# Attention over memory keys: a key tile of the sample comes in four transfers to all 128 partitions in place of two to 64 partitions each

## The chip, the core and the metric

The kernel runs on one core of one Trainium2 chip. The metric is the device time of one execution in microseconds (us); each execution loads all inputs from the chip's memory and stores all outputs. One step holds a prompt of 256 tokens and 8 sample sequences of 8 tokens, so 320 tokens in all, with a model width of 2048. All arrays are float32.

## What is computed

One layer of a hybrid decoder: a mixer (a state space scan and a short convolution), an attention over 256 memory tokens, and a lookup of experts (PEER), each added to the residual. The change touches the attention over the memory alone:

```python
def mem_attend(xn, k, v, wq, wo):
    b, L, _ = xn.shape
    q = (xn @ wq).reshape(b, L, MEM_HEADS, MEM_HEAD_DIM)
    s = jnp.einsum('blhd,bmhd->bhlm', q, k.astype(q.dtype)).astype(jnp.float32) * (1.0 / math.sqrt(MEM_HEAD_DIM))
    p = jax.nn.softmax(s, axis=-1)
...
```

There are 4 heads of 512 columns. The prompt's keys and values are computed by this kernel (stored as outputs `p_mem_k`, `p_mem_v`, and read back); those of the 8 sample sequences come from the inputs `cache_mem_k` and `cache_mem_v`, 256 tokens x 4 heads x 512 columns for each sequence. So one head of one sequence has a key block of 256 x 512 numbers, 512 KB, of which a row of 2 KB lies every 8 KB in memory.

## The kernel before

The program is one stream of work for the engines. TensorE (PE), VectorE (DVE) and ScalarE (ACT) run in an order that the kernel writes out by hand; the order of GpSimd (POOL), which in this stage only issues DMA transfers, is chosen by the framework's scheduler. Weights come through SyncE's own queue (SP).

In the attention stage the loop runs over four heads. A head has nine key tiles (eight of the sample, one of the prompt) and nine value tiles. Between them stand pieces of the projection of the next head's queries, and in the last head of the output projection (`between`, L1503 to L1507); the matmuls of these pieces are `pg` at L1214 to L1216.

A key or value tile is `kv`, 128 partitions x 1024 numbers (512 KB), made and loaded by `kv_load` (L1122). There are ten buffers (KVT): seven in a pool of their own, three in pool `PQ`. So a load waits until the tile ten places earlier has been used: a key tile is free after VectorE's transpose (`turned`, L1361 to L1363, written to `tt`), a value tile after TensorE's matmuls (L1448).

`kv_load(src, blocks)` has three forms. Sample keys (called at L1153 for the first head and at L1396 for the others) have `blocks` 2: two transfers, one for each half of the 512 columns, each to 64 partitions. Prompt keys (L1368) have `blocks` 4: four transfers to 32 partitions each. Values (L1368 and L1433) have `blocks` 0: one transfer to all 128 partitions. Sample keys and prompt keys are issued at L1129, values at L1132.

After the load VectorE transposes a key tile in blocks of 32 x 32 (L1363), TensorE multiplies it with the queries into the scores `pss` (sample, L1408) or, after a split in two parts, `psp` (prompt, L1424 to L1426), a softmax follows on a side stream, and the values are multiplied into `pso` (sample, L1448) and `po` (prompt, L1466 to L1468). L248 on ScalarE and L249 on VectorE make the two parts (H and L) of a float32 operand, for weights `W` as for keys. When the attention is done, POOL loads the residual again (`XN`, L1497), which was stored at L1157 (`x_d<-XF`).

The first eight key loads are queued before the stage (`open_kv`, L1149 to L1153): seven of them go out from 886 to 917 us, while the mixer's output projection runs, and the eighth at 1140 us.

Of other transfers on POOL the text names these: the stores of `row` at L740, of which the first four (417.9 to 420.3 us) read 3 partitions and write 72 runs of 32 numbers each, in the list of order 72x1x32; the loads and stores of the scan's state, `SB` (L778, L926, 128x8x128), and `EE` (L702, 64x16x64).

Of the kernel before, what the change touches and what calls it, by code (L numbers as in the profile page):

```python
# [23 lines left out]
TS = 64  # L24
# [139 lines left out]
def step(ctx, tc, ins, outs, dbg=None, stop=None):  # L164
    nc = tc.nc
# [956 lines left out]
    def kv_load(src, blocks):  # L1122
        def load():
            own = next(tiles) % KVT < KV1
            t = (KV if own else PQ)["pool"].tile([P, 1024], F32, tag="kv", bufs=KV1 if own else KVT - KV1, name="kv")
            if blocks:
                n, p = 512 // blocks, P // blocks
                for e in range(blocks):
                    nc.gpsimd.dma_start(t[p * e:p * e + p].rearrange("p (a d) -> p a d", d=n),  # L1129
                                        src[:, n * e:n * e + n].rearrange("(a p) d -> p a d", p=p))  # L1130
            else:
                nc.gpsimd.dma_start(t.rearrange("p (m d) -> p m d", m=2), src.rearrange("(m p) d -> p m d", p=P))  # L1132
            ready.append(t)
        loads.append(load)
# [1145 lines left out]
```

## Time and profile before

| quantity | value |
|---|---|
| time of three executions | 3087.83, 3092.4, 3096.58 us |
| median | 3092.4 us |
| time of the profiled execution | 3088.27 us |
| its span | 3086.5 us |
| granted TensorE clock over the span | 0.997 |
| attention stage, from the first prompt key load to the last value's matmul | 1141 to 1352 us |
| DMA traffic, mean over the span | 295 GB/s |

The profile is one execution. PE, DVE, ACT, POOL and SP are the engines TensorE, VectorE, ScalarE, GpSimd and SyncE; PEld is TensorE's loading of weights. The span is the time from the first to the last instruction; the execution's time is a little longer. A row of a group or of a timeline names the line of the program, the engine, the operation, and output <- input; in brackets or after the last bar stands how long the engine was idle before it, and the instruction or DMA whose end released it. `in_cache_mem_k_dram` and `in_cache_mem_v_dram` are the caches of the sample; `out_dram` as an input is the prompt's keys or values. A row of a DMA issue gives the KB of one transfer and the median time from issue to landing, in us. The granted clock is TensorE's, as a share of full speed.

### The profile page before, as it was taken

How to read it: one execution, taken by the hardware profiler on the slowest of the kernel's cores; microseconds unless marked ns; L12 is line 12 of the kernel's file. 1: busy time of each engine (PE TensorE's matmuls, PEld its weight loads, DVE VectorE, ACT ScalarE, POOL GpSimd, SP SyncE). 2: the span in 40 equal slices, each digit the busy share in tenths (PEclk: the TensorE clock that was granted, in tenths of full speed). 3: DMA queues.
4: the chain of work that ended last, by engine and by line, in shares of the span. 5: the costliest groups of instructions: out<-in, count | busy, mean ns of one | idle time of the engine just before them, and what ended most of it. 6: DMA issues, size and time to landing. Idle time of an engine off the chain costs nothing.

```text
span 3086.5 us, 55315 instructions
## 1 busy us (share of the span) xinstructions
PE 3051.7 (99%) x19709; PEld 2794.0 (91%) x19709; DVE 2275.2 (74%) x4477; ACT 1589.5 (51%) x3202; POOL 1359.7 (44%) x1500
## 2 busy tenths in 40 slices
PE   8999999999999999999999999999999999999998
PEld 7889999999999999889999999888888888888886
DVE  5556866666566456656778899988885889888886
ACT  5545643434554443444554444766674545555555
POOL 0011221111110002310458999989887656555553
PEclk9999999999999999999999999999999999999999
DMA  8888899899999858975966788879998999999996
GB/s 275 288 270 308 302 331 333 304 330 307 357 320 353 292 186 228 261 235 159 244 201 223 287 319 316 304 290 319 336 331 264 344 331 361 338 345 334 332 305 220
DMA packets 445321, 909.19 MB, mean 295 GB/s; under 512 B 43336, under 2 KB 252400, under 8 KB 419572
## 3 DMA queue, kind: packets, MB, share of 16 engines
q1 hardware_dynamic: 316372, 543.31, 51.3%
q0 software_dynamic: 60656, 227.34, 22.4%
q10 hardware_dynamic: 68016, 135.01, 12.8%
q8 instruction: 154, 2.52, 0.3%
q14 instruction: 123, 1.01, 0.1%
HBM read 849.44 MB, written 190.05 MB: 337 GB/s over the span
## 4 chain that ended last, share of the span: by engine, by line
PE 84%; issue 4%; DMA 3%; POOL 3%; DVE 3%; ACT 1%; SPq 0%; DVEq 0%; POOLq 0%; ACTq 0%
PE pg L371 11%; PE pg L372 11%; PE pg L373 11%; PE pu L1998 7%; PE acc L2173 6%; PE acc L2174 6%; PE acc L2172 6%; PE pu L1999 4%; POOL L L1979 3%; PE pu L2005 2%; PE pu L2004 2%; PE pu L2003 2%; PE pgate L1901 2%; PE pg L1214 2%; PE pg L319 1%
## 5 line engine op out<-in xcount | busy, mean ns | idle before, releaser
L249 DVE TENSOR_TENSOR L<-W,H 128x512 fp32r<-128x512 f32 x1312 | 899.2, 711 | 341.0 <-ACT H L248 332.0
L248 ACT ACTIVATE H<-W 128x512 fp32r<-128x512 f32 x1312 | 795.9, 628 | 679.6 <-PE acc L2174 234.7
L1979 POOL TENSOR_TENSOR L<-tt,H 128x512 fp32r<-128x512 f32 x511 | 646.8, 1298 | 60.7 <-ACT H L1976 50.0
L371 PE MATMUL pg<-AH,H 128*128 128x320 f32 x1856 | 581.7, 313 | 0.0
L373 PE MATMUL pg<-AH,L 128*128 128x320 f32 x1856 | 573.6, 309 | 0.0
L372 PE MATMUL pg<-AL,H 128*128 128x320 f32 x1856 | 573.4, 309 | 0.0
L2172 PE MATMUL acc<-H,wt 128*128 128x512 f32 x1024 | 398.5, 389 | 1.1 <-DVE at L2012 1.1
L2173 PE MATMUL acc<-L,wt 128*128 128x512 f32 x1024 | 398.8, 389 | 0.6 <-DVE L L249 0.5
L2174 PE MATMUL acc<-H,wt 128*128 128x512 f32 x1024 | 398.4, 389 | 0.0
L1976 ACT ACTIVATE H<-tt 128x512 fp32r<-128x512 f32 x512 | 309.0, 626 | 144.8 <-DVE tt L1967 120.0
L1967 DVE STREAM_TRANSPOSE tt<-W 128x512 f32<-128x512 f32 x512 | 338.1, 691 | 58.9 <-POOL L L1979 55.7
L1998 PE MATMUL pu<-XP,H 128*128 128x512 f32 x1035 | 371.2, 399 | 0.0
L371 PEld LDWEIGHTS pg<-AH,H 128*128 128x128 f32 x1856 | 349.0, 188 | 2.1 <-issue 0.5
L372 PEld LDWEIGHTS pg<-AL,H 128*128 128x128 f32 x1856 | 348.7, 188 | 1.8
L373 PEld LDWEIGHTS pg<-AH,L 128*128 128x128 f32 x1856 | 348.4, 188 | 0.0
L1999 PE MATMUL pu<-XP,L 128*128 128x256 f32 x1104 | 297.0, 279 | 0.3 <-POOL L L1979 0.3
L2121 POOL TENSOR_TENSOR at<-at,G 128x108 f32<-128x108 f32 x192 | 168.4, 891 | 252.0 <-DMA at<-act_d 205.0
L2005 PE MATMUL pu<-XP,L 128*128 128x256 f32 x944 | 269.4, 285 | 3.0 <-POOL L L1979 2.7
L2003 PE MATMUL pu<-XP,H 128*128 128x256 f32 x944 | 267.8, 284 | 0.1
L2004 PE MATMUL pu<-XP,H 128*128 128x256 f32 x944 | 267.0, 283 | 0.0
L1998 PEld LDWEIGHTS pu<-XP,H 128*128 128x128 f32 x1035 | 194.3, 188 | 39.9
L2173 PEld LDWEIGHTS acc<-L,wt 128*128 128x128 f32 x1024 | 192.2, 188 | 42.0 <-DVE L L249 2.1
(496 smaller groups left out, 5810.3 us busy)
## 6 DMA issues: line engine op xcount, KB each, us to landing
u_d<-in_peer_u_dram ACTq DMA_DIRECT2D x128, 1024.0 KB, 8.4
W<-u_d SPq DMA_DIRECT2D x128, 1024.0 KB, 6.6
W<-in_peer_v_dram SPq DMA_DIRECT2D x256, 512.0 KB, 6.4
W<-in_w_in_dram SPq DMA_DIRECT2D x176, 512.0 KB, 7.4
W<-in_w_out_dram SPq DMA_DIRECT2D x64, 512.0 KB, 6.5
W<-in_w_mem_k_dram SPq DMA_DIRECT2D x32, 512.0 KB, 5.9
W<-in_w_mem_v_dram SPq DMA_DIRECT2D x32, 512.0 KB, 5.6
kv<-in_cache_mem_k_dram POOLq DMA_DIRECT2D x64, 256.0 KB, 9.0
```

The costliest lines, as they stand in the source:

```text
L248: S.activation(h, src, AF.Copy)
L249: V.tensor_tensor(l, src, h.bitcast(F32), ALU.subtract)
L371: PE.matmul(out, hv[:, j, c0:c1], ah[:, k, 0:n], start=st, stop=False)
L372: PE.matmul(out, hv[:, j, c0:c1], al[:, k, 0:n], start=False, stop=False)
L373: PE.matmul(out, lv[:, j, c0:c1], ah[:, k, 0:n], start=False, stop=sp)
L1967: V.transpose(tt.rearrange("p (k a i) -> p k a i", a=4, i=32), box["x", i].rearrange("p (a k j) -> p k a j", a=4, k=16)[:, 4 * q:4 * q + 4])
L1979: G.tensor_tensor(l, src, h.bitcast(F32), ALU.subtract)
L1998: PE.matmul(*wide, start=k == 0, stop=False)
L1999: PE.matmul(pu[:, 0:TP], lv[:, j], PP["xp"][:, 0, k], start=False, stop=False)
L2172: PE.matmul(out, th, h, start=i == 0, stop=False)
L2173: PE.matmul(out, th, l, start=False, stop=False)
L2174: PE.matmul(out, tl, h, start=False, stop=i == P - 1)
```

## The change

`kv_load` gets a form of its own for `blocks` 2. A sample key tile now comes in four transfers in place of two. The tile's contents stay the same: partition 64 e + p, column 256 a + d holds row 64 a + p, column 256 e + d of the key block.

```diff
--- before.py
+++ after.py
@@ -1123,7 +1123,11 @@
         def load():
             own = next(tiles) % KVT < KV1
             t = (KV if own else PQ)["pool"].tile([P, 1024], F32, tag="kv", bufs=KV1 if own else KVT - KV1, name="kv")
-            if blocks:
+            if blocks == 2:
+                for a in range(4):
+                    nc.gpsimd.dma_start(t[:, 256 * a:256 * a + 256],
+                                        src[TS * a:TS * a + TS].rearrange("p (e d) -> e p d", e=2))
+            elif blocks:
                 n, p = 512 // blocks, P // blocks
                 for e in range(blocks):
                     nc.gpsimd.dma_start(t[p * e:p * e + p].rearrange("p (a d) -> p a d", d=n),
```

| | before | after |
|---|---|---|
| transfers of one sample key tile | 2 | 4 |
| bytes of one transfer | 256 KB | 128 KB |
| partitions written by one | 64 | 128 |
| runs of 1 KB per partition in one | 4 | 1 |
| source of one, outermost first | 64 rows, 4 row blocks, 256 numbers | 2 column halves, 64 rows, 256 numbers |

(TS is 64.) There are 32 sample key tiles. Lines behind L1125 of the program move down by four: the transfers of sample keys are at L1128 after the change, of prompt keys at L1133, of values at L1136. PE, DVE, ACT and SP keep their order, but for the numbers in the names of tiles.

On POOL each transfer waits for a semaphore of a ring of eight (DMASW0 to DMASW7), that is for the landing of the transfer eight places before it; the first transfer of a tile also waits for the engine that used the buffer (DVE or PE). Among the first keys of the last head, before the change (names: `kv` is a tile, the second name the input, then partitions x runs x numbers of one run as the list shows the tile's side):

```order
L1129 DMA kv_14285<-in_cache_mem_k_dram 64x4x256 [waits DMASW2_49,DVE_49]
L1129 DMA kv_14285<-in_cache_mem_k_dram 64x4x256 [waits DMASW3_49]
L1132 DMA kv_14344<-in_cache_mem_v_dram 128x2x512 [waits DMASW4_49,PE_49]
L1132 DMA kv_14354<-in_cache_mem_v_dram 128x2x512 [waits DMASW5_49,PE_49]
L1129 DMA kv_14379<-in_cache_mem_k_dram 64x4x256 [waits DMASW6_49,DVE_49]
L1129 DMA kv_14379<-in_cache_mem_k_dram 64x4x256 [waits DMASW7_49]
L1132 DMA kv_14402<-out_6_dram 128x2x512 [waits DMASW0_49,PE_49]
L1129 DMA kv_14439<-in_cache_mem_k_dram 64x4x256 [waits DMASW1_49,PE_49]
L1129 DMA kv_14439<-in_cache_mem_k_dram 64x4x256 [waits DMASW2_49]
```

After the change, at the same place:

```order
L1128 DMA kv_14433<-in_cache_mem_k_dram 128x1x256 [waits DMASW2_49,DVE_49]
L1128 DMA kv_14433<-in_cache_mem_k_dram 128x1x256 [waits DMASW3_49]
L1128 DMA kv_14433<-in_cache_mem_k_dram 128x1x256 [waits DMASW4_49]
L1136 DMA kv_14398<-in_cache_mem_v_dram 128x2x512 [waits DMASW5_49,PE_49]
L1136 DMA kv_14408<-in_cache_mem_v_dram 128x2x512 [waits DMASW6_49,PE_49]
L1128 DMA kv_14433<-in_cache_mem_k_dram 128x1x256 [waits DMASW7_49]
L1136 DMA kv_14458<-out_6_dram 128x2x512 [waits DMASW0_49,PE_49]
L1128 DMA kv_14495<-in_cache_mem_k_dram 128x1x256 [waits DMASW1_49,PE_49]
L1128 DMA kv_14495<-in_cache_mem_k_dram 128x1x256 [waits DMASW2_49]
L1128 DMA kv_14495<-in_cache_mem_k_dram 128x1x256 [waits DMASW3_49]
L1128 DMA kv_14495<-in_cache_mem_k_dram 128x1x256 [waits DMASW4_49]
L1128 DMA kv_14517<-in_cache_mem_k_dram 128x1x256 [waits DMASW5_49,DVE_49]
```

The three keys from kv_14433 on now pass through the ring in four steps each; two value loads that stood ahead of both steps of a key (kv_14344, kv_14354) stand ahead of its last step (kv_14398, kv_14408 ahead of the fourth of kv_14433).

The last two sample keys of the last head, before the change (the tile kv_14564 is the last one; two value loads follow, then the prompt's keys):

```order
L1132 DMA kv_14504<-in_cache_mem_v_dram 128x2x512 [waits DMASW6_49,PE_49]
L1129 DMA kv_14533<-in_cache_mem_k_dram 64x4x256 [waits DMASW7_49,PE_49]
L1129 DMA kv_14533<-in_cache_mem_k_dram 64x4x256 [waits DMASW0_49]
L1129 DMA kv_14564<-in_cache_mem_k_dram 64x4x256 [waits DMASW1_49,DVE_49]
L1129 DMA kv_14564<-in_cache_mem_k_dram 64x4x256 [waits DMASW2_49]
L1132 DMA kv_14581<-in_cache_mem_v_dram 128x2x512 [waits DMASW3_49,PE_49]
L1132 DMA kv_14615<-in_cache_mem_v_dram 128x2x512 [waits DMASW4_49,PE_49]
L1129 DMA kv_14643<-out_5_dram 32x8x128 [waits DMASW5_49,DVE_49]
L1129 DMA kv_14643<-out_5_dram 32x8x128 [waits DMASW6_49]
```

And after it:

```order
L1136 DMA kv_14564<-in_cache_mem_v_dram 128x2x512 [waits DMASW2_49,PE_49]
L1128 DMA kv_14593<-in_cache_mem_k_dram 128x1x256 [waits DMASW3_49,PE_49]
L1128 DMA kv_14593<-in_cache_mem_k_dram 128x1x256 [waits DMASW4_49]
L1128 DMA kv_14593<-in_cache_mem_k_dram 128x1x256 [waits DMASW5_49]
L1128 DMA kv_14593<-in_cache_mem_k_dram 128x1x256 [waits DMASW6_49]
L1128 DMA kv_14626<-in_cache_mem_k_dram 128x1x256 [waits DMASW7_49,DVE_49]
L1128 DMA kv_14626<-in_cache_mem_k_dram 128x1x256 [waits DMASW0_49]
L1128 DMA kv_14626<-in_cache_mem_k_dram 128x1x256 [waits DMASW1_49]
L1128 DMA kv_14626<-in_cache_mem_k_dram 128x1x256 [waits DMASW2_49]
L1133 DMA kv_14707<-out_5_dram 32x8x128 [waits DMASW3_49,DVE_49]
L1133 DMA kv_14707<-out_5_dram 32x8x128 [waits DMASW4_49]
L1136 DMA kv_14645<-in_cache_mem_v_dram 128x2x512 [waits DMASW5_49,PE_49]
```

Between two value loads stand eight steps of keys where four stood, which is the whole ring; the first prompt key step stands directly behind the last sample key, ahead of two value loads that stood before it.

## The prediction

> **What bounds the kernel now.** First the page's busy times and the windows of the attention stage.
>
> ```profile
> PE 3051.7 (99%) x19709; PEld 2794.0 (91%) x19709; DVE 2275.2 (74%) x4477; ACT 1589.5 (51%) x3202; POOL 1359.7 (44%) x1500
> ...
> 1140.00:1200.00 60.00, 60.00 (x503) 57.24 (x502) 36.93 (x70) 25.17 (x50) 14.69 (x24) 1.00 0.87 242
> 1200.00:1250.00 50.00, 49.37 (x447) 42.46 (x447) 33.05 (x56) 22.21 (x55) 17.50 (x27) 1.00 0.81 224
> 1250.00:1300.00 50.00, 49.29 (x469) 41.44 (x467) 31.97 (x55) 19.58 (x48) 17.52 (x27) 1.00 1.04 271
> 1300.00:1350.00 50.00, 43.68 (x378) 33.46 (x377) 27.73 (x48) 19.86 (x45) 16.18 (x24) 0.90 0.93 286
> ```
>
> A window's columns are its length, then busy PE, PEld, DVE, ACT, POOL, the granted clock, the DMA share and GB/s. TensorE is the bound: it is idle 0.63, 0.71 and 6.32 us in the last three windows and never in the first. So the changed loads can gain only in the last, and can lose wherever they make TensorE wait. What ended the waits, from the waits of PE over the stage, its timeline and VectorE's:
>
> ```profile
> PE pss L1408 <- DVE tt L1363: 3.2, 1, 3.2
> PE pg L1215 <- DVE AL L249: 2.9, 1, 2.9
> ...
> 1321.69 0.47 PE L1216 MATMUL pg<-AH,L 128*128 128x320 f32 x1
> 1326.83 0.31 PE L1216 MATMUL pg<-AH,L 128*128 128x320 f32 x1
> ...
> 1306.07 1.25 DVE L1363 STREAM_TRANSPOSE tt<-kv 128x1024 f32<-128x1024 f32 x1 [0.29 <-DMA kv<-in_cache_mem_k_dram]
> 1315.46 1.25 DVE L1363 STREAM_TRANSPOSE tt<-kv 128x1024 f32<-128x1024 f32 x1 [4.46 <-DMA kv<-in_cache_mem_k_dram]
> 1318.46 1.25 DVE L1363 STREAM_TRANSPOSE tt<-kv 128x1024 f32<-128x1024 f32 x1 [1.75 <-DMA kv<-in_cache_mem_k_dram]
> ```
>
> The first wait is TensorE's for a transposed key tile, and that transpose had waited 4.46 us for a key load; the second is for a split behind the next late transpose (VectorE runs in order). Both are the key load. They cost 3.2 + 2.9 = 6.1 us. Then the clock: over those 50 us it was 0.90, which is 0.10 x 50 / 0.5 = 10 us at half speed (the same matmul 0.47 us instead of 0.31); less the 2.9 us idle among them, 7 us of work ran at half and lost 3.5 us. **If the key loads came early, 6.1 + 3.5 = 9.6 us would go; that is the most this change can gain.** The chain of waits, in order of time, says why the load is late:
>
> ```profile
> 1303.13 0.61 POOL kv L1129
> 1303.75 14.59 DMA kv<-in_cache_mem_k_dram
> 1318.52 1.11 issue
> ```
>
> It was issued at 1303 and took 14.6 us. It could not be issued earlier: in the list of order each load waits for the landing of the one eight places before it. Eight transfers are in flight at most, so a stretch of n transfers with landing time L takes n x L / 8.
>
> **What is unchanged.** VectorE, ScalarE, TensorE and SyncE keep their instructions and order; bytes and destinations are the same. Three things change: issues on POOL, how a transfer is dealt to the DMA engines and memory, and the number of loads in that line of eight.
>
> **1. Issues.** 32 sample key tiles, two more transfers each, 64 in all. The page's groups and the lines of POOL by form have these durations:
>
> ```profile
> L1129 POOL DMA_DIRECT2D kv<-in_cache_mem_k_dram x64 | 39.7, 627 | 90.7 <-DVE tt L1363 41.6 <-DVE XS L1076 23.2 <-PE pt L241 8.9
> L1132 POOL DMA_DIRECT2D kv<-in_cache_mem_v_dram x32 | 22.9, 717 | 62.4 <-DVE tt L1363 32.4 <-PE pso L1448 14.5 <-DMA kv<-in_cache_mem_k_dram 5.8
> L926 POOL DMA_DIRECT2D out_dram<-SB x16 | 14.6, 915 | 104.4 <-DVE SB L922 99.1 <-DVE L L249 5.4
> L1129 POOL DMA_DIRECT2D kv<-out_dram x16 | 9.4, 591 | 10.9 <-DMA kv<-in_cache_mem_k_dram 4.1 <-DVE AL L249 3.2 <-DVE tt L1363 1.8
> L1157 POOL DMA_DIRECT2D x_d<-XF x8 | 4.4, 548 | 217.2 <-DVE XF L1113 217.2
> ...
> L702 POOL DMA_DIRECT2D EE<-acs_d x2 | 1.7, 834 | 2.1 <-DMA acs_d<-ACS 2.1
> ...
> L740 POOL DMA_DIRECT2D out_dram<-row x4 | 2.6, 665 | 0.0
> ```
>
> (The last row is of the window 417.8 to 420.3 us.) The new load moves 128 runs of 1 KB, as many runs as x_d<-XF (128x640), which gives 0.55 us; the upper end is the dearest of these rows, 0.92 (SB, 1024 runs). A key tile's issue goes from 1.25 us to between 2.2 and 3.7. I take 0.87, the mean of the two dear rows (834 and 915), for the reason of part 2. A pair (key and V tile) is then 4 x 0.87 + 0.72 = 4.2 us of POOL. A pair's share of the stage is (1324.2 − 1156.8) / 36 = 4.65 us by the first and last transpose:
>
> ```profile
> L1363 DVE STREAM_TRANSPOSE tt<-kv x36: 1225/1239/1247, 1156.8 to 1324.2; 128x1024 f32<-128x1024 f32 x36
> ```
>
> So issuing alone fits, barely. Nothing but these loads (and four loads of XN behind them) stands on POOL here.
>
> **2. The landing.** Two rows of DMA traffic, a stretch with key loads alone and one with V loads (all 128 partitions), and the issues with their median landing:
>
> ```profile
> DMA packets 124, 0.39 MB, mean 193 GB/s; under 512 B 30, under 2 KB 30, under 8 KB 124
> ...
> DMA packets 312, 1.15 MB, mean 384 GB/s; under 512 B 31, under 2 KB 31, under 8 KB 312
> ...
> DMA packets 917, 2.56 MB, mean 256 GB/s; under 512 B 95, under 2 KB 95, under 8 KB 916
> ...
> kv<-in_cache_mem_k_dram POOLq DMA_DIRECT2D x64, 256.0 KB, 9.0
> kv<-in_cache_mem_v_dram POOLq DMA_DIRECT2D x32, 512.0 KB, 9.2
> x_d<-XF POOLq DMA_DIRECT2D x8, 320.0 KB, 2.5
> ```
>
> (In order 1164 to 1166, 1342 to 1345 and 1300 to 1310 us.) Keys into 64 partitions moved at 193 GB/s, V at 384: the old shape is half as fast, and this speaks for the change. The Trainium skill, "SBUF — State Buffer", section "Door 1: The DMA port swizzle", has it so: 64 consecutive partitions reach only 8 of 16 ports. By that rule alone the key's half of a pair would take half the time, which is the rival "spread" below.
>
> Against it: the new source runs over two column halves first, then 64 rows, so its outermost count is 2, where the old one had 64 on both sides. The four stores of `row` in that window have an outermost count of 3, and 72 short runs cost 665 ns to issue, where 256 runs of a prompt key load (outermost 32) cost 591 and 128 runs of x_d<-XF 548. Fewer runs cost more. It fits if the issue is paid by runs per DMA engine, and `row` goes to 3 engines: 8 per engine 548, 16 per engine 591 and (old keys) 627, 24 per engine 665, 64 per engine 834 (EE) and 915 (SB). (V's 717 has longer runs.) So I take the new load to be dealt to **two of the 16 engines**, 64 runs or 64 KB each. The Trainium skill, "DMA: Bandwidth & Descriptors", section "Why a DMA increments its semaphore by 16 and not by 1", states such a rule: the number of engines is the largest up to 16 that divides the slowest dimension of both sides, here 2; it also tells of exceptions for direct copies issued from POOL, and no row here shows this shape.
>
> An engine's share is 384 / 16 = 24 GB/s at best and 256 / 16 = 16 in the crowded stretch. Landing is a fixed part, the 64 KB, and what lies before them on that engine: a V tile's 32 KB, at worst another key share of 64 KB. For the fixed part I take the 2.5 us of x_d<-XF as its upper bound. So 2.5 + 96 / 24 = 6.5 us below, 2.5 + 160 / 16 = 12.5 above; I take the middle, **9.5 us**, close to the 9.0 of a key load now. (Below that still, as for evenly dealt loads, 128 of 320 KB of the 2.5 row.)
>
> **3. The line of eight.** The stretch in which POOL hardly waits for buffers, 1231 to 1304 us:
>
> ```profile
> L1129 POOL DMA_DIRECT2D kv<-in_cache_mem_k_dram x30 | 18.7, 630 | 24.2 <-DVE tt L1363 9.1 <-PE pso L1448 5.0 <-DMA kv<-in_cache_mem_v_dram 3.2
> L1132 POOL DMA_DIRECT2D kv<-in_cache_mem_v_dram x10 | 7.2, 721 | 18.1 <-DMA kv<-in_cache_mem_v_dram 4.8 <-PE pso L1448 4.0 <-DVE tt L1363 3.9
> L1129 POOL DMA_DIRECT2D kv<-out_dram x4 | 2.4, 594 | 2.3 <-DMA kv<-in_cache_mem_k_dram 2.3
> L1132 POOL DMA_DIRECT2D kv<-out_dram x2 | 1.4, 718 | 2.8 <-PE pso L1448 2.8
> ```
>
> Before: 46 transfers in 73 us, of which POOL waited about 25 us for buffers (9.1 + 5.0 + 4.0 + 3.9 + 2.8). After: 30 more, 76 transfers, 76 x 9.5 / 8 = 90 us, 17 more. The 25 us of buffer waits are no full cover: a tile's buffer comes free when a later instruction than today's has run; I keep a third of them, 8 us. The stall of before stays inside these sums, since its last loads are as late. Sum 25 us. Clock: before 6.1 us of waits cost 3.5 at half speed; of 25 us of waits at that ratio 14, but a slow TensorE also hides part of the next late load, so I take a third, 5 us. **Sum: +30 us.** At the ends: landing 6.5 gives 76 x 6.5 / 8 = 62 us, no new wait, and the old one goes: −9.6. Landing 12.5 gives 119, that is +46, with 8 and 9 of the other terms +63. V loads stand behind four key transfers in place of two; values are used after the scores, and the list of order shows two V loads slipped ahead of a tile's last quarter, so this is in the same line and is not counted again. The loads of the first seven keys (887 to 930) have over 240 us until their transposes at 1156.8: nothing.
>
> **Against the time.** The profiled execution took 3088.3 us (span 3086.5), 4.1 below the median of 3092.4. 3088 + 30 = 3118; on the median 3122. I say **3120**.
>
> **Rivals.**
> - *Spread over all engines.* If the 128 runs go to 16 engines, at 384 GB/s in place of 193, the landing falls to about 5 us (9.0 x 193 / 384 = 4.5), POOL's pair to 4 x 0.55 + 0.72 = 2.9 us, 76 x 5 / 8 = 48 us: the stall goes. 3092 − 9.6 = **3083**, on the edge of what a measurement can tell (0.3%, 9 us). For it speaks the 384 row; against it the 72 dear runs. Chance 0.13, half of it over the edge.
> - *Two engines but hidden.* Landing about 8: 76 us, +3 in the stretch; the buffer waits cover it, and the stall at 1311 to 1320 stays as it is: **3092**, between 3085 and 3100. For it: eight loads on eight different pairs would keep all 16 engines busy. Chance 0.13.
> - *Slower by POOL itself.* The issue at 0.92 and more becomes the bound: from 4.65 − 0.72 = 3.93 us per key tile, 0.98 us an issue, POOL is late in every pair. At 1.2 us (a third over the dearest row) 36 pairs lose 36 x (5.5 − 4.65) = 31 us, less some 10 of lead: +20, **3112**. Against it: no row of a plain transfer is that dear. Chance 0.06.
> - *Much slower.* Key loads in flight fall on the same pair of engines, landing 15 us and more: 76 x 15 / 8 = 142, +70 and clock: **3170**. Chance 0.08.
>
> **How the numbers follow.** Forecast 0.60. Slower by over 0.3%: 0.60 + 0.06 + 0.08, 0.74; within: 0.13 and half of the spread case, 0.18; faster 0.08. The likeliest case's own range is 3103 to 3155 (its 12.5 end lies above that, its 6.5 end is the rival). The range goes from 3086 to 3160: it leaves out the spread case and the much slower one, about 0.2.
>
> **What would show it.** In the changed profile: the mean of the key issue (0.55 spread, 0.87 two engines); the landing of 128 KB (5 or 9.5 us); GB/s from 1230 to 1320 below the 224 to 286 of before; the waits of PE for tt at L1363's new place, several of them from 1240 on instead of one; the granted clock below 1.00 in more than one window. Wrong would be the forecast if key loads land within 7 us while the windows up to 1300 keep TensorE idle under 1 us.

## The result and the profile after

The changed kernel takes 3127.4 us (median of 5 runs, 3125.4 to 3128.5) against 3092.8 us (5 runs): 1.0116 times as long, interval 1.0100 to 1.0132, or 35 us slower. The profiled execution took 3128.1 us, its span 3126.4. First the windows (880 to 930 of before and of after, then after through the attention stage), columns as above:

```profile
880.00:930.00 50.00, 50.00 (x339) 49.42 (x339) 32.00 (x56) 24.85 (x46) 8.59 (x14) 1.00 1.05 339
```

```profile
880.00:930.00 50.00, 47.02 (x307) 46.21 (x306) 29.39 (x51) 24.95 (x47) 18.95 (x24) 0.97 1.10 310
1200.00:1250.00 50.00, 49.15 (x459) 42.88 (x459) 29.36 (x47) 18.65 (x42) 22.05 (x29) 1.00 1.04 234
1250.00:1300.00 50.00, 43.43 (x372) 36.77 (x371) 24.77 (x43) 16.42 (x40) 25.81 (x34) 0.93 1.05 207
1300.00:1350.00 50.00, 34.85 (x277) 26.14 (x276) 20.16 (x35) 14.50 (x37) 29.38 (x38) 0.86 1.04 194
1350.00:1400.00 50.00, 43.21 (x326) 34.83 (x327) 25.67 (x44) 18.56 (x39) 13.94 (x21) 0.87 0.90 291
```

TensorE, which was idle 7.0 us from 1250 to 1350, is now idle 28.5 us from 1250 to 1400 (6.6, 15.2, 6.8). From 1300 to 1350 the DMA share is 1.04 where it was 0.93, but 194 GB/s are moved where it was 286. Full and slow is the sign to look for. Part of the fullness is a new kind of packet, of 16 bytes (experiment 2): by the trace's single packets these make 0.21 of the 1.04, so that without them the share would be 0.83. At 880 to 930, where TensorE never waited, 3 us are gone too. TensorE's longest waits from 880 to 1420:

```profile
PE pg L1218 <- DVE ql L249: 7.5, 2, 5.3
PE pg L1219 <- DVE AL L249: 5.1, 1, 5.1
PE pss L1412 <- DVE tt L1367: 4.2, 1, 4.2
PE po L1472 <- DVE L L249: 3.6, 1, 3.6
```

Only one is for a transposed key itself. The longer ones are for splits that VectorE does right behind late transposes: it starts `ql` at 1318.0 behind the transpose of 1316.8, and `AL` at 1342.5 behind that of 1341.3, which had waited 1.8 and 2.6 us for keys.

The groups of POOL's issues and the landings:

```profile
L1128 POOL DMA_DIRECT2D kv<-in_cache_mem_k_dram x128 | 101.6, 801 | 120.6 <-DMA kv<-in_cache_mem_k_dram 66.3 <-DMA kv<-in_cache_mem_v_dram 18.1 <-DVE tt L1367 17.0
...
kv<-in_cache_mem_k_dram POOLq DMA_DIRECT2D x128, 128.0 KB, 10.8
kv<-in_cache_mem_v_dram POOLq DMA_DIRECT2D x32, 512.0 KB, 12.1
```

A key transfer of half the bytes costs more to issue (801 ns where it was 627) and lands later (10.8 us where it was 9.0), and it takes V along (12.1 where it was 9.2). Before its issue POOL now waits, over the whole kernel, for landings (66 + 18 us) where it waited for free buffers (DVE tt, 17 us now, 42 before): the bound has moved from the consumer to the line of eight.

VectorE's timeline (the last four transposes of sample keys), and the end of the chain of waits:

```profile
1336.89 1.25 DVE L1367 STREAM_TRANSPOSE tt<-kv 128x1024 f32<-128x1024 f32 x1 [4.63 <-DMA kv<-in_cache_mem_k_dram]
1341.31 1.25 DVE L1367 STREAM_TRANSPOSE tt<-kv 128x1024 f32<-128x1024 f32 x1 [2.60 <-DMA kv<-in_cache_mem_k_dram]
1350.18 1.25 DVE L1367 STREAM_TRANSPOSE tt<-kv 128x1024 f32<-128x1024 f32 x1 [6.45 <-DMA kv<-in_cache_mem_k_dram]
1355.46 1.25 DVE L1367 STREAM_TRANSPOSE tt<-kv 128x1024 f32<-128x1024 f32 x1 [4.03 <-DMA kv<-in_cache_mem_k_dram]
```

```profile
1306.14 10.57 DMA kv<-in_cache_mem_k_dram
...
1323.06 1.82 POOL kv L1128 x3
1325.48 11.29 DMA kv<-in_cache_mem_k_dram
1337.05 1.60 POOL kv L1128 x2
1338.92 11.13 DMA kv<-in_cache_mem_k_dram
1350.62 0.71 POOL kv L1136
```

Six of the last head's eight transposes of sample keys wait for their keys, the last four of them 2.6 to 6.5 us each. From 1325 on the chain goes from landing to landing, about 11 us each, with a few issues between. It is not the line of eight alone: from 1317 to 1323 (left out at the "...") the chain passes through VectorE and TensorE, which still held the buffer of the next load.

### The profile page after: what moved, and what is told of

Its sections match the earlier page's. It is cut to its first block, busy times and chain, and to the rows that moved or that the text cites. A ratio compares the mean times of both kernels' runs of the same rounds, so it can differ in the third digit from the quotient of the medians.

```text
span 3126.4 us, 55401 instructions
## 1 busy us (share of the span) xinstructions
PE 3064.6 (98%) x19709; PEld 2803.1 (90%) x19709; DVE 2272.3 (73%) x4477; ACT 1588.3 (51%) x3202; POOL 1416.6 (45%) x1564
## 2 busy tenths in 40 slices
DMA packets 475017, 909.65 MB, mean 291 GB/s; under 512 B 73032, under 2 KB 282096, under 8 KB 449268
## 4 chain that ended last, share of the span: by engine, by line
PE 77%; DMA 10%; issue 4%; DVE 4%; POOL 3%; ACT 1%; SPq 0%; DVEq 0%; POOLq 0%; ACTq 0%
PE pg L371 11%; PE pg L372 10%; PE pg L373 10%; PE pu L2002 8%; PE acc L2177 5%; PE acc L2178 5%; PE acc L2176 5%; PE pu L2003 4%; DMA kv<-in_cache_mem_k_dram 3%; POOL L L1983 2%; PE pu L2009 2%; PE pu L2008 2%; PE pu L2007 2%; PE pgate L1905 2%; DMA gv<-in_peer_v_dram,EV 2%
## 5 line engine op out<-in xcount | busy, mean ns | idle before, releaser
L248 ACT ACTIVATE H<-W 128x512 fp32r<-128x512 f32 x1312 | 796.3, 628 | 698.4 <-PE acc L2178 236.5
## 6 DMA issues: line engine op xcount, KB each, us to landing
kv<-in_cache_mem_k_dram POOLq DMA_DIRECT2D x128, 128.0 KB, 10.8
```

Source lines behind the costliest of these rows:

```text
L248: S.activation(h, src, AF.Copy)
```

## Experiments

The theory: a load whose source has an outermost count of 2 goes to two DMA engines. The rivals: the number of transfers in the line of eight ("count"), and the destination of 128 partitions with one run each ("shape"). The edits of experiments 1, 2 and 4 replace the body of the new form in `kv_load`. In them e is a column half and m a row half: `e, m = a % 2, a // 2`. Times are medians, ratios against runs of the kernel before on the same chip.

**1. Count alone.** Four transfers to 64 partitions, rows outermost.

```diff
-nc.gpsimd.dma_start(t[:, 256 * a:256 * a + 256],
-                    src[TS * a:TS * a + TS].rearrange("p (e d) -> e p d", e=2))
+nc.gpsimd.dma_start(t[TS * e:TS * e + TS, 512 * m:512 * m + 512].rearrange("p (a d) -> p a d", d=256),
+                    src[P * m:P * m + P, 256 * e:256 * e + 256].rearrange("(a p) d -> p a d", p=TS))
```

> Four transfers of 128 KB per sample key tile as in the change, but each to 64 partitions with the 64 rows outermost in the source (64x2x256). Theory (a transfer with an outermost count of 2 goes to two DMA engines): issue falls to about 0.55 us, landing below 8 us, the time within 10 us of before (3083 to 3103). Rival 'count' (eight places in the line, four steps a key): POOL and the line of eight as in the change, about 3120 to 3130. Rival 'shape' (it is the 128 partitions with one run each that are slow): near before as well.

Measured 3085.5 beside 3088.3 us, ratio 0.9991 (0.9978 to 1.0003); issue 600 ns, landing 6.9 us. Twice as many transfers cost nothing when each is spread: the landing falls as the transfers get smaller. "Count" falls as a cause by itself.

**2. Outermost count.** The same transfers to 128 partitions with one run each; only the source is read in another order. `rows_first` takes 128 rows of one column half (the first + line); the others take those rows in g groups, with g = 2, 4, 8, 16 (the second + line for g = 2).

```diff
-                    src[TS * a:TS * a + TS].rearrange("p (e d) -> e p d", e=2))
+                    src[P * m:P * m + P, 256 * e:256 * e + 256])
+                    src[P * m:P * m + P, 256 * e:256 * e + 256].rearrange("(r g) d -> g r d", g=2))
```

> The same four transfers to 128 partitions (128x1x256), but the source's outermost dimension is 128 rows of one column half in place of two column halves. The rows of a key tile are then placed otherwise than the transpose wants them, so the scores are not the reference's; bytes, runs, count and destination are those of the change. Theory (two engines): issue about 0.55 us, landing 5 to 6 us, the late-key stall of before gone, 3080 to 3090. Rivals 'count' and 'shape': as the change, 3120 to 3130.

> As rows_first, but the 128 rows are taken as two groups (even rows, then odd rows), so the outermost count is 2 again, without column halves; the rows are placed otherwise than the transpose wants. Theory (two engines): as the change, issue 0.80 us, landing about 11 us, 3120 to 3135. If the two column halves of a row were what is slow: as rows_first, about 3085.

> As groups2 with eight groups of 16 rows: outermost count 8. Theory (as many engines as the outermost count divides, up to 16): 16 runs per engine, issue about 0.60 us as the prompt keys' 0.59, landing 6 to 7 us, 3080 to 3095. Rivals 'count' and 'shape': as the change.

> As groups2 with four groups of 32 rows: outermost count 4, four DMA engines with 32 runs each by the theory. Issue between the 0.61 us of eight and the 0.80 us of two, about 0.68; landing 8 to 9.5 us; the loss of the late heads mostly gone, since 76 x 8.7 / 8 = 83 us in the stretch from 1231 to 1304 against 76 x 11 / 8 = 105 for two: 3090 to 3105. If the loss belongs to an outermost count of 2 alone: as groups8, 3088.

> As groups2 with sixteen groups of 8 rows: outermost count 16, all DMA engines by the theory, rows taken in a strided order. Theory: as rows_first, issue about 0.55 us, landing about 5.4 us, 0.997 to 0.999 of before (3079 to 3085 beside a before of 3088). If the strided order of rows was what groups8 lost against rows_first: as groups8, 0.9997.

| outermost count | kernel | ratio (interval) | mean issue, ns | median landing, us | small packets more than before |
|---|---|---|---|---|---|
| 2 | the change | 1.0116 (1.0100 to 1.0132) | 801 | 10.8 | 29,696 |
| 2 | groups2 | 1.0118 (1.0091 to 1.0145) | 802 | 11.8 | 29,696 |
| 4 | groups4 | 1.0055 (1.0038 to 1.0072) | 686 | | 13,312 |
| 8 | groups8 | 0.9997 (0.9985 to 1.0008) | 611 | 7.4 | 5,121 |
| 16 | groups16 | 0.9985 (0.9976 to 0.9995) | 546 | | 1,024 |
| 128 | rows_first | 0.9980 (0.9970 to 0.9990) | 543 | 5.4 | 1,024 |

(The profiles of groups4 and groups16 give no landing. Small packets are those under 512 bytes.) The last column comes from the profiles' lines of all packets; before, the change, groups8 and rows_first:

```profile
DMA packets 445321, 909.19 MB, mean 295 GB/s; under 512 B 43336, under 2 KB 252400, under 8 KB 419572
```

```profile
DMA packets 475017, 909.65 MB, mean 291 GB/s; under 512 B 73032, under 2 KB 282096, under 8 KB 449268
```

```profile
DMA packets 450442, 909.26 MB, mean 295 GB/s; under 512 B 48457, under 2 KB 257521, under 8 KB 424693
```

```profile
DMA packets 446345, 909.19 MB, mean 295 GB/s; under 512 B 44360, under 2 KB 253424, under 8 KB 420596
```

The keys' bytes, their runs, the number of transfers and the destination are the same in all six; the rows stand in another place than the transpose wants in all but the change, so the other five do the same work on other scores. The time follows the outermost count alone, with no difference between the column halves of the change and the even and odd rows of groups2, so both rivals fall. groups16 and rows_first agree within their intervals: the strided order of rows is not what groups8 lacks. The small packets say how the transfers are dealt. 64 more transfers with 16 packets each are the 1,024 of rows_first. Above that the change has (73,032 − 44,360) / 128 = 224 per transfer = 14 x 16, and groups8 (48,457 − 44,360) / 128 = 32 = 8 x 4: as many engines left over as the theory says, 14 of 16 and 8 of 16, each with as many small packets as a busy engine has packets of 4 KB (64 KB are 16 of them, 16 KB are 4). They hold 16 bytes each: 0.46 MB more (909.65 − 909.19) in 28,672 packets. No view shows a single engine's queue; that the small packets sit on the idle engines is inferred from these products.

The trace's single packets show the concentration itself. In groups2 the 4 KB packets of the first key transfer that is issued at 886 us start 0, 0.17, 0.24, 0.40, 0.47, 0.64, 0.71 and 0.87 us after the first of them: two rows, each with a step of 0.235 us, and for 1.2 us never more than two packets at once. In the change it is the same for the first 0.6 us; in rows_first up to ten are under way in that time. From 880 to 960 us, while any key packet is under way, there are 3.6 of them on average in the change and 3.3 in groups2, 4.3 with a count of 4, 6.4 with 8, and 7.1 and 7.2 with 16 and 128.

What stays open is how much of the loss is the concentration and how much the small packets, which come with it in every kernel here. From 1231 to 1347 us the trace of the change gives the small packets 0.155 of a share of 1.055.

rows_first also shows what 128 partitions are worth where all engines are used. In two stretches with key loads alone (1164 to 1166 us), before and in rows_first:

```profile
DMA packets 124, 0.39 MB, mean 193 GB/s; under 512 B 30, under 2 KB 30, under 8 KB 124
...
q0 software_dynamic: 124, 0.39, 94.0%
```

```profile
DMA packets 170, 0.46 MB, mean 229 GB/s; under 512 B 58, under 2 KB 58, under 8 KB 170
...
q0 software_dynamic: 170, 0.46, 67.7%
```

With 64 partitions the engines are 94% busy at 193 GB/s; with 128, 68% at 229, so full engines would move 229 / 0.68 = 338 by proportion, an estimate. The four spread transfers to 64 partitions of experiment 1 took 3085.5 us on the same chip, rows_first 3082.7: about half of the 6 us goes with the destination; whether the smaller transfers give the rest is not clear of noise. And the late stall of before is gone: TensorE is busy 48.95 of the 50 us from 1300 where it was busy 43.68.

```profile
1300.00:1350.00 50.00, 48.95 (x443) 38.80 (x442) 29.50 (x52) 21.86 (x50) 17.16 (x26) 1.00 0.91 302
```

**3. Where the loss arises.** The four transfers for the first head's keys alone, and for the other heads' alone: `blocks` 1 stands for the new form here and 2 for the old one; first_head has the first piece of the edit alone, later_heads the second alone.

```diff
-            kv_load(cache_k[0, b, :, 0], 2)
+            kv_load(cache_k[0, b, :, 0], 1)
...
-                kv_load(cache_k[0, b, :, h], 2)
+                kv_load(cache_k[0, b, :, h], 1)
```

> Only the first head's eight key tiles come in the four transfers of the change; the other 24 as before. Theory: the first seven loads (issued 886 to 939 us) take DMA engines from the output projection's weights and cost what the profile after shows there, about 5 us, and the attention stage loses nothing: +5 us, 3092 to 3098 beside a before of about 3091. Rival 'only the attention stage' (as the prediction had it): no change. Rival 'a shift there is taken back later': no change.

> Only the key tiles of heads two to four (24 of 32) come in four transfers; the first head's as before. Theory: the rest of the loss, about 30 us, 3117 to 3126. Rival (the early loads start a delay that the attention stage carries on): about 3100.

first_head: 3092.5 beside 3087.6, ratio 1.0021 (1.0008 to 1.0033), +6 us by the ratio. later_heads: 3123.2, ratio 1.0107 (1.0087 to 1.0128), +33. Together 39 beside the change's 36, equal within the intervals. So the first head's loads, seven of which run under the output projection, cost 6 us; in the trace of first_head TensorE is busy 46.87 of the 50 us from 880, as it is in the change (47.02). The DMA traffic from 886 to 960 us, before and after, shows where they come from:

```profile
DMA packets 17696, 26.26 MB, mean 355 GB/s; under 512 B 718, under 2 KB 10897, under 8 KB 17690
...
kv<-in_cache_mem_k_dram POOLq DMA_DIRECT2D x14, 256.0 KB, 9.8
```

```profile
DMA packets 22440, 23.88 MB, mean 323 GB/s; under 512 B 7167, under 2 KB 16354, under 8 KB 22434
...
kv<-in_cache_mem_k_dram POOLq DMA_DIRECT2D x28, 128.0 KB, 17.9
```

The keys have over 200 us to spare there, but the weights that share the engines do not: 2.4 MB fewer are moved in the same 74 us, and ScalarE's first step on a weight, `H L248`, waits 30.4 us for `W<-in_w_out_dram` in 895 to 960 where it waited 23.9. Whether two full engines or the small packets on the others hold the weights back is not separated.

**4. Half the transfers, each on two engines.** Two transfers of 128 rows with all 512 columns, even rows then odd. m counts the row halves.

```diff
-for a in range(4):
-    nc.gpsimd.dma_start(t[:, 256 * a:256 * a + 256],
-                        src[TS * a:TS * a + TS].rearrange("p (e d) -> e p d", e=2))
+for m in range(2):
+    nc.gpsimd.dma_start(t[:, 512 * m:512 * m + 512],
+                        src[P * m:P * m + P].rearrange("(r g) d -> g r d", g=2))
```

> Two transfers of 256 KB per sample key tile, as many as before, to 128 partitions, each with an outermost count of 2 (even rows, odd rows) and 128 runs of 2 KB; the rows are placed otherwise than the transpose wants, so the scores are not the reference's. Theory (two engines, 128 KB on each): issue about 0.8 us, landing 15 to 19 us, per pair 3 x 17 / 8 = 6.4 us as against 5 x 11 / 8 = 6.9 with four: 3115 to 3135. Rival (the loss comes from four places in the line of eight in place of two): near before, 3085 to 3095.

3108.4 beside 3087.6 us, ratio 1.0075 (1.0056 to 1.0093), +23; issue 806 ns. Below what the theory gave (3115 to 3135), far above "count" (3085 to 3095). With as many transfers as before the concentration costs two thirds of the whole; the last third comes with four in place of two of them, which count alone (experiment 1) does not cost. Its runs are 2 KB and not 1 KB, which may make some of the difference; this was not separated. The issue speaks for runs per engine and not for small packets: 64 runs per engine cost 806 ns here with (72,008 − 43,336) / 64 = 448 small packets a transfer, and 801 in the change with 224. In all these are 28,672, as many as the change has; so their number alone does not set the loss, which is 23 us here and 36 there.

**5. Can the gain of rows_first be had with the right placement?** Two tries with the old loads, the half for partitions 64 to 127 issued on SyncE's queue so that both halves can be written at once: for all heads (sp_half), and for the last head alone (sp_last). The edit is shortened: `...` stands for the arguments, which stay, and sp_last does it only where h is 3.

```diff
-for e in range(2): nc.gpsimd.dma_start(...)
+for e, q in ((0, nc.gpsimd), (1, nc.sync)): q.dma_start(...)
```

> The two transfers of before, but the one to partitions 64 to 127 is issued on SyncE's queue, between its weight loads, so that both halves of the partitions can be written at once and POOL's line of eight holds half as many key transfers. Theory: the landing on POOL falls to 6 to 7 us and the stall at 1311 to 1320 goes, 3080 to 3088, if SyncE does not hold weights back behind a key load that waits for its buffer; if it does, 3100 and more.

> The kernel before, but in the last head alone the transfer of each sample key to partitions 64 to 127 is issued on SyncE's queue in place of POOL's, where the late keys were. Theory (the late loads wait for places in POOL's line of eight and for half of the partitions at a time): the landing there falls, some or all of the 9.6 us of the late stall goes, 3080 to 3087 beside a before of 3089, ratio 0.997 to 0.9995. If the weights held back on SyncE cost as much: within 2 us of before.

sp_half 3089.6 beside 3087.6, ratio 1.0008 (0.9998 to 1.0017); sp_last 3088.2 beside 3087.3, ratio 0.9998 (0.9982 to 1.0014). No gain either way, where the theory had 3080 to 3088 and 3080 to 3087. In sp_last TensorE's wait for the transposed keys is gone, but a new one stands close by, from the waits of PE:

```profile
PE psm L1315 <- ACT SC L1308: 3.3, 1, 3.3
```

Nothing tried beats the kernel before with the reference's output. A layout with whole rows in 128 partitions could use rows_first's loads, but needs another arrangement of the queries and twice as many matmuls of half the width; it was not tried.

## Why the prediction was right

Right in sign, place and mechanism, and close in size: +28 us against the median was predicted (+30 by the sum), 35 came. That the size came so close is partly luck: several terms were off, and not all the same way.

- **What bounds, and the most to gain.** Confirmed: rows_first, which lets the late keys come early, gains 0.2% (3082.7 beside 3088.3 us, 6 us); the sum had 9.6. Its share for the clock was too large by its own rows: matmuls of 0.47 us in place of 0.31 lose a third of 7 us, 2.4, and not 3.5. The spread rival was right about what spreading does (issue 543 ns, landing 5.4 us in rows_first), wrong only about this change. The rule of the Trainium skill on "Door 1: The DMA port swizzle" ("SBUF — State Buffer") agrees with rows_first (229 GB/s at 68% busy where 64 partitions gave 193 at 94%), and is not enough here.
- **Issues.** 801 ns measured, 870 taken, 548 to 915 as bounds. Issue cost by runs per engine is confirmed by the curve: 543 and 546 ns at 8 runs, 611 at 16, 686 at 32, 801 and 802 at 64. It is not the whole of the cost: the transfers of experiment 1 have 8 runs per engine too and cost 600. The inference from the dear stores of `row` held.
- **Two engines.** Confirmed by groups2, by the curve, and by the single packets, which run in two rows. The rule on the number of engines in the Trainium skill ("DMA: Bandwidth & Descriptors", "Why a DMA increments its semaphore by 16 and not by 1") agrees for every count measured, with 64 and 32 runs an engine at 2 and 4; no exception for direct copies from POOL showed.
- **Landing: the term that was too small.** 9.5 us taken, 10.8 measured (6.5 to 12.5 as bounds). In the sum 76 x 10.8 / 8 = 103 us in place of 90, and V's landing of 12.1 as well. In the trace of after, 81 of these transfers are issued from 1231 to 1347: 116 us, or 11.5 us of landing by the line of eight. The sum's own 76 take 107 us (1240.7 to 1347.3) where the 46 of before took 72, so 35 us more; the sum had 17 + 8 = 25.
- **"The stall of before stays inside these sums": not whole.** The last sample key is issued 42.7 us later than before (1346.5 beside 1303.7) but transposed only 37.0 us later (1355.5 beside 1318.5): its load no longer takes 14.6 us, and about 6 us come back.
- **Buffer waits and clock.** A third of the 25 us of buffer waits was kept, 8 us. In that stretch POOL still waits about 9 us for buffers. The clock: 0.93, 0.86 and 0.87 in three windows are 34 us at half speed. TensorE is busy for 24 of them, so they do not lie mostly in its waits. By matmuls of 0.47 us in place of 0.31 that work loses about 8 us, some 6 more than before and near the 5 taken; how much of it hides later waits is not separated.
- **The step that was wrong: "the loads of the first seven keys: nothing".** It asked only whether those keys come in time. first_head shows +6 us (1.0021): the weights of the output projection come later.
- **The terms together.** With 10.8 us of landing the sum would be +43, with the first head +49, where 35 were measured. About 14 us of it did not come; 6 of them are the load above, and the rest is not separated.
- **The signs.** The issue, the landing, the GB/s and the clock came as told. "Several" waits for `tt` did not: there is one, of 4.2 us, and the late keys reach TensorE mostly through VectorE's splits (7.5 and 5.1 us).
- **Rivals.** "Hidden" is out: 3127 us lies above its 3100, and keys land after 10.8 us and not 8. "Slower by POOL itself" is out: the issue was cheaper than taken, and POOL waits for landings. "Much slower" is out: in the stretch the landing was 11.5 us by the line of eight, not 15 and more.

The attention stage by itself, by VectorE's timeline, the tenth key tile's transpose (the first of the second head) before and after:

```profile
1205.30 1.25 DVE L1363 STREAM_TRANSPOSE tt<-kv 128x1024 f32<-128x1024 f32 x1
```

```profile
1210.43 1.25 DVE L1367 STREAM_TRANSPOSE tt<-kv 128x1024 f32<-128x1024 f32 x1
...
1362.42 1.25 DVE L1367 STREAM_TRANSPOSE tt<-kv 128x1024 f32<-128x1024 f32 x1 [3.62 <-DMA kv<-out_dram]
```

The last one, at 1362.4, stood at 1324.2 before: the delay grows from 5.1 to 38.2 us, by 33 us, which is what later_heads costs. Profiles of two executions differ by a few us elsewhere (39.9 us between these two, 35 between the medians).

## What to carry to other kernels

Before reshaping a DMA to reach more partitions, look at the outermost count on both sides: 2 there cost 1.2% of this kernel, 16 gained 0.15% with the same bytes, runs and destination. A DMA share near 1 with falling GB/s, an issue time that rises while the runs per transfer fall, and thousands of new packets under 512 bytes are how it shows. And a load with much time to spare still costs what it takes from the loads beside it.

## What was not expected of the hardware

A transfer on few engines brings small packets with it, by the products above on the other engines: 224 for each transfer with an outermost count of 2, 96 with 4 ((56,648 − 44,360) / 128), 32 with 8, none with 16. They hold 16 bytes here, and 8 in groups2_two (0.23 MB more in 28,672 packets). The trace of the change gives them 0.21 of the DMA share from 1300 to 1350 us; what they cost the kernel by themselves was not measured. And two transfers to disjoint halves of the partitions from two queues (sp_half, sp_last) did not shorten the kernel, though the loads of before, in halves, move at 193 GB/s where V's move at 384.
